# A decoder trunk: weight sums moved from VectorE to accumulating DMAs, and one set of transposes placed earlier

## The chip, the cores and the metric

The kernel runs on one NeuronCore of a Trainium2 chip. TensorE (PE) does matmuls and transposes, VectorE (DVE) and ScalarE (ACT) elementwise work, GpSimd (POOL) small scalar steps; SyncE (SP) issues DMAs and POOL issues others. Each engine takes its instructions in order from a queue of its own and waits on semaphores. The metric is the device time of one execution in microseconds. The time before is 2124.06 us, the median of three runs (2122.8 to 2125.29).

## The reference

Two layers, each of three residual steps with a layer norm behind them, on 512 positions of width 1024 in float32:

```python
for l in range(DEPTH):
    x = layer_norm(ALPHA * x + 0.5 * swiglu(x, ffn1_w13[l], ffn1_w2[l]), ln_g[l, 0], ln_b[l, 0])
    m = mixer(x, w_in[l], ...)
    x = layer_norm(ALPHA * x + m, ln_g[l, 1], ln_b[l, 1])
    x = layer_norm(ALPHA * x + 0.5 * swiglu(x, ffn2_w13[l], ffn2_w2[l]), ln_g[l, 2], ln_b[l, 2])

def swiglu(x, w13, w2):
    a, b = jnp.split(x @ w13, 2, axis=-1)
    return (jax.nn.silu(a) * b) @ w2          # inner width 2816
```

`mixer` projects x to eight parts, runs a gated linear recurrence on some and a gated spatial mixing on others, projects both branches, merges them by sigmoids and ends with one output projection.

## The kernel before

**Float32 products in three passes.** Every operand is split (`split`, L117) into a rounded high part, made by ScalarE (L118), and the rest, made by VectorE (L119). A product of two operands is then three matmuls: high by high, high by low, low by high. `weights` (L121) loads 128 x 1024 weights (512 KB) with SP into one of four `raw` buffers and splits them into two of ten `w` tiles.

**A SwiGLU stage** (`ffn`, L444) runs over 22 column blocks j of 128 inner columns. For each it loads two weight blocks, `a` and `b`, and computes `pa` and `pb` (`proj`, L143), 24 matmuls of 512 columns each; `glu` multiplies silu(`pa`) with `pb` and stores the result in quarters. Blocks j and j + 11 make one block k of the second product, and when the second of them is done, `activation_sums(k)` and `weight_sums(k)` follow. The order of k is 8, 9, 10, then 0 to 7.

**The second product** (class `Seven`) is a 2 x 2 block product with seven instead of eight block multiplications (Strassen's scheme in Winograd's form). It needs sums of the quarters of the second weights, `w2`: t1 = q0 + q1, t3 = q2 + q1, t2 = q0 + t3 and t4 = q3 + t2, where q0 to q3 are the four 128 x 512 quarters as they lie in DRAM. `weight_sums` (L278) loads them with SP into two tiles, `ra_w` and `rb_w`, forms the four sums on VectorE (L284, L289) and stores each with a DMA on POOL's queue (L285, L290) to the DRAM tiles `t1`, `t2` and `t34`. The tag of `ra_w` and `rb_w` has two buffers, so the next block's loads wait until this block's stores have landed. `run` (L331) later loads quarters and sums (`two`, L345) as `r_b`, `r_t`, `r_c` and `r_d`, splits and multiplies them.

**Between stages.** At the end of a stage four rows of 128 positions are finished one after the other. `norm` (L187) normalises a row (a square sum on ScalarE, two small steps on POOL, two on VectorE) and hands out `to_features` (L155), which transposes it on TensorE into `xh` and `xl`, the operands of the next stage. The next stage's first two pairs of blocks are computed in two halves of 256 columns: the first half needs rows 0 and 1, the second rows 2 and 3 (`need`, L209).

**What sets the order.** The class `Flow` keeps a clock in ns that advances by 216 per matmul of 512 columns as matmuls are written. Side work is a generator with a due time: `flow.add(gen, delay)` makes it due `delay` ns from now, each `tick` runs one due step, and `finish` runs what is left. Row transposes are due `LN_NS` = 11500 ns behind their `norm`. The program so written is then compiled, and the scheduler may set an instruction ahead of others on its engine where its operands allow it; semaphores keep the dependences.

Of the kernel before, what the change touches and what calls it, by code (L numbers as in the profile page):

```python
# [27 lines left out]
F32 = mybir.dt.float32  # L28
# [3 lines left out]
ALU = mybir.AluOpType  # L32
# [50 lines left out]
def trunk(ctx: ExitStack, tc, x_in, xt_in, w13, w2, w_in, w_br, w_out, ln_g, ln_b, lb_in, hgn, sgg, sgb, sgws,  # L83
# [37 lines left out]
    def weights(src, name, early=False):  # L121
# [8 lines left out]
        return hi, lo  # L130

    NW = 10
    NS, NRAW, NSA = 33, 4, 3
# [52 lines left out]

    def norm(t, xt, sums, g, b, last):  # L187

# [12 lines left out]
        if not last:  # L201
            x_at[t] = dram.tile([P, D], F32, name=f"xd{t}", tag=f"xd{t}", bufs=2)
            nc.gpsimd.dma_start(x_at[t], xt)
            ready[t] = flow.add(to_features(t, xt), LN_NS)

    LN_NS = 11500.0
    ready = [None] * NT
# [7 lines left out]
    def out_proj(nk, lhs, w_of, c, ln, tag):  # L215
# [23 lines left out]
        for t in range(NT):  # L239
            sums = small("sums", 2)  # L240
            for q in range(2):
                for k in range(nk - tail, nk):
                    unit(k, t, (q,))
                add_to(xs[t], q, c, ys[t][q], sums)
            norm(t, xs[t], sums, g, b, False)

# [12 lines left out]
    class Seven:  # L259
# [5 lines left out]
        def __init__(self, w_of):  # L265
            self.w_of = w_of
            self.r, self.t, self.last = {}, {}, None
            self.t1 = [dram.tile([P, 512], F32, name=f"t1{k}", tag=f"t1{k}", bufs=1) for k in range(NH2)]
            self.t2 = [dram.tile([P, 2, 512], F32, name=f"t2{k}", tag=f"t2{k}", bufs=1) for k in range(0, NH2, 2)]
            self.t34 = [dram.tile([P, 2, 512], F32, name=f"t34{k}", tag=f"t34{k}", bufs=1) for k in range(NH2)]  # L270

# [6 lines left out]
        def weight_sums(self, k):  # L278
# [5 lines left out]
            V.tensor_tensor(t1, a[:, 0], a[:, 1], op=ALU.add)  # L284
            nc.gpsimd.dma_start(self.t1[k], t1)  # L285
            for to, dst, u, v in ((self.t34[k][:, 0], a[:, 1], b[:, 0], a[:, 1]),
                                  (self.t2[k // 2][:, k % 2], a[:, 0], a[:, 0], a[:, 1]),
                                  (self.t34[k][:, 1], b[:, 1], b[:, 1], a[:, 0])):
                V.tensor_tensor(dst, u, v, op=ALU.add)  # L289
                nc.gpsimd.dma_start(to, dst)  # L290
# [40 lines left out]
        def run(self, c, ln, last):  # L331
# [45 lines left out]
            for k in ks:  # L377
                two(f"b{k}", [self.w_of(k)[:, 0], self.t1[k]], [("B11", k), ("t1", k)])
                if k % 2 == 0:
# [35 lines left out]
            for k in range(4):  # L415
                two(f"d{k}", [self.t34[k]], [("t3", k), ("t4", k)], True)
            if not last:
# [10 lines left out]
            for k in ks:  # L428
                if k >= 4:
                    two(f"d{k}", [self.t34[k]], [("t3", k), ("t4", k)])  # L430
                if k < NH2 - tail:
                    for ps, p in ((E, P7), (F, P4)):
                        for tt in range(2):
                            mm(ps, p, [k], tt, True, True)
# [8 lines left out]

    def ffn(l, i, last=False, first_of_all=False):  # L444
        made = list(range(Seven.KEPT, NH2)) + list(range(Seven.KEPT))
        seven = Seven(lambda k: w2[l, i, k])
        js = [j for k in made for j in (k, k + NH2)]
# [10 lines left out]
        def glu(j, args):  # L458
# [6 lines left out]
            if a:  # L465
                seven.activation_sums(k)
                seven.weight_sums(k)

# [9 lines left out]
        for z, j in enumerate(js[start:]):  # L478
# [9 lines left out]
            pair_of(j, args, 0, T)  # L488
            glu(j, args)
        seven.run(0.5 / ALPHA, (l, 2 * i), last)  # L490

# [375 lines left out]
    for l in range(DEPTH):  # L867
        ffn(l, 0, first_of_all=(l == 0))
        if l == 0:
            flow.finish(prep)  # L870
        mixer(l, lb, om)
        ffn(l, 1, last=(l == DEPTH - 1))

# [97 lines left out]
```

## Time and profile before

| what | us |
|---|---|
| median of three runs | 2124.06 |
| the profiled execution, its own time | 2122.98 |
| its span, first to last instruction | 2120.1 |
| TensorE busy in the span | 2097.9 |
| TensorE waiting for `xh` (3 times) | 11.0 |

The span has this course: in the first layer the first SwiGLU's blocks until about 262 us, its second product to about 357, the mixer to about 707, the second SwiGLU's blocks to about 950 and its second product to 1060; then the second layer in the same way. In a row of a timeline stand the start in us, the duration, engine, line, operation, output and inputs, shape and count, and in brackets how long the engine idled before and what ended it. SPq rows are DMA issues on SP; a DMA issue on POOL is an instruction of about 0.54 us. In a row of DMA issues the last two figures are the size and the median time from issue to landing. In a row of windows stand the busy time of each engine with its count, the granted clock, the DMA engines' busy share and GB/s.

### The profile page before, as it was taken

The page shows a single profiled execution, that of the slowest core. Times are in us where ns is not written, and L with a number is a line of the kernel's source. Part 1 is how long each engine was busy: PE and PEld are TensorE (multiplying, and loading weights), DVE is VectorE, ACT ScalarE, POOL GpSimd, SP SyncE. Part 2 cuts the span into 40 slices and gives each one's busy share as a digit, 9 for nine tenths or more (in the row PEclk, how much of TensorE's full clock was granted, in tenths as well). Part 3 has the DMA queues.
Part 4 walks back from the last instruction along what each step waited for, and adds up shares of the span by engine and source line. Part 5 has one row for each costly group of instructions (what it writes and reads, how often), then busy time and mean ns, then how long its engine had stood idle before and what let it go on. Part 6 is the DMA issues. An engine that isn't in the chain of part 4 may idle for free.

```text
span 2120.1 us, 26533 instructions
## 1 busy us (share of the span) xinstructions
PE 2097.9 (99%) x10024; PEld 1761.5 (83%) x10024; DVE 1226.6 (58%) x2019; ACT 772.2 (36%) x1090; POOL 214.6 (10%) x360
## 2 busy tenths in 40 slices
PE   8999999999999999999999999999999999999998
PEld 6888888888888888888898888888888888888886
DVE  5545578843535644548754456779344456454586
ACT  4222455224322422226522234552333324222363
POOL 0101002001000110101111010020010001110101
PEclk9999999999999999999999999999999999999999
DMA  7665777122242465557757557761222426655674
GB/s 268 215 209 179 251 254 263 42 80 80 82 157 90 162 235 185 192 207 275 249 186 235 179 203 237 273 227 42 89 89 89 141 90 202 211 192 201 224 262 143
DMA packets 113905, 381.01 MB, mean 180 GB/s; under 512 B 14321, under 2 KB 14577, under 8 KB 113777
## 3 DMA queue, kind: packets, MB, share of 16 engines
q1 hardware_dynamic: 88848, 291.68, 42.0%
q0 software_dynamic: 24928, 87.64, 10.9%
q8 instruction: 78, 1.28, 0.2%
q14 instruction: 51, 0.41, 0.1%
HBM read 311.11 MB, written 68.16 MB: 179 GB/s over the span
## 4 chain that ended last, share of the span: by engine, by line
PE 80%; DVE 2%; ACT 1%; DMA 1%; POOL 0%; issue 0%; POOLq 0%; DVEq 0%; ACTq 0%
PE pa L143 17%; PE pb L143 16%; PE z L143 8%; PE pA L341 4%; PE pC L341 4%; PE y L143 4%; PE y L226 3%; PE pF L341 2%; PE q L143 2%; PE pE L341 2%; PE f L143 2%; PE pB L341 2%; PE i L551 2%; PE g L143 2%; PE v L551 2%; PE u L143 2%
## 5 line engine op out<-in xcount | busy, mean ns | idle before, releaser
L143 PE MATMUL pa<-xh,h_a 128*128 128x512 f32 (+1 forms) x752 | 285.0, 379 | 11.2 <-ACT xh L118 11.0
L143 PE MATMUL pa<-xl,h_a 128*128 128x512 f32 (+1 forms) x752 | 284.6, 378 | 0.1
L143 PE MATMUL pa<-xh,l_a 128*128 128x512 f32 (+1 forms) x752 | 283.7, 377 | 0.0
L143 PE MATMUL pb<-xh,h_b 128*128 128x512 f32 (+1 forms) x752 | 283.1, 377 | 0.0
L143 PE MATMUL pb<-xh,l_b 128*128 128x512 f32 (+1 forms) x752 | 282.4, 376 | 0.3 <-DVE l_b L119 0.3
L143 PE MATMUL pb<-xl,h_b 128*128 128x512 f32 (+1 forms) x752 | 282.4, 375 | 0.0
L119 DVE TENSOR_TENSOR l_b<-r_b,h_b 128x1024 fp32r<-128x1024 f32 x132 | 161.5, 1224 | 166.4 <-ACT h_b L118 165.8
L118 ACT ACTIVATE h_b<-r_b 128x1024 fp32r<-128x1024 f32 x132 | 139.9, 1060 | 303.6 <-PE pa L143 245.4
L463 DVE TENSOR_TENSOR r<-sa,pb 128x512 f32<-128x512 f32 x88 | 60.5, 688 | 303.3 <-PE pb L143 303.3
L118 ACT ACTIVATE h_a<-r_a 128x1024 fp32r<-128x1024 f32 (+1 forms) x89 | 93.5, 1051 | 278.9 <-PE pb L143 264.2
L143 PEld LDWEIGHTS pa<-xh,h_a 128*128 128x128 f32 x752 | 142.9, 190 | 38.4 <-ACT xh L118 12.6
L143 PEld LDWEIGHTS pa<-xl,h_a 128*128 128x128 f32 x752 | 142.2, 189 | 28.0 <-DVE xl L119 2.3
L143 PEld LDWEIGHTS pa<-xh,l_a 128*128 128x128 f32 x752 | 142.4, 189 | 25.6
L143 PEld LDWEIGHTS pb<-xl,h_b 128*128 128x128 f32 x752 | 141.7, 188 | 25.8
L143 PEld LDWEIGHTS pb<-xh,l_b 128*128 128x128 f32 x752 | 141.6, 188 | 26.1 <-DVE l_b L119 0.8
L143 PEld LDWEIGHTS pb<-xh,h_b 128*128 128x128 f32 x752 | 141.7, 188 | 25.5
L119 DVE TENSOR_TENSOR l_a<-r_a,h_a 128x1024 fp32r<-128x1024 f32 (+1 forms) x89 | 107.7, 1210 | 16.2 <-ACT h_a L118 12.3
L143 PE MATMUL z<-xh,h_z 128*128 128x512 f32 x256 | 102.6, 401 | 0.0
L285 POOL DMA_DIRECT2D t<-t x44 | 23.9, 543 | 763.8 <-DVE t L284 697.5
L143 PE MATMUL z<-xh,l_z 128*128 128x512 f32 x256 | 99.8, 390 | 0.0
L143 PE MATMUL z<-xl,h_z 128*128 128x512 f32 x256 | 99.8, 390 | 0.0
L119 DVE TENSOR_TENSOR l_z<-r_z,h_z 128x1024 fp32r<-128x1024 f32 x32 | 39.2, 1225 | 72.5 <-ACT h_z L118 72.4
(270 smaller groups left out, 4246.5 us busy)
## 6 DMA issues: line engine op xcount, KB each, us to landing
r_b<-in_w_dram SPq DMA_DIRECT2D x88, 512.0 KB, 4.7
r_a<-in_w_dram SPq DMA_DIRECT2D x87, 512.0 KB, 4.7
ra_w<-in_w_dram SPq DMA_DIRECT2D x44, 512.0 KB, 5.5
rb_w<-in_w_dram SPq DMA_DIRECT2D x44, 512.0 KB, 5.2
t<-ra_w POOLq DMA_DIRECT2D x88, 256.0 KB, 2.6
r_c<-in_w_dram SPq DMA_DIRECT2D x44, 512.0 KB, 6.3
r_d<-t SPq DMA_DIRECT2D x44, 512.0 KB, 4.6
r_z<-in_w_in_dram SPq DMA_DIRECT2D x32, 512.0 KB, 3.5
```

What stands on the lines that cost most here:

```text
L118: S.activation(hi, src, AF.Copy)
L119: V.tensor_tensor(lo, src, hi.bitcast(F32), op=ALU.subtract)
L143: PE.matmul(ps[:, n0:n0 + n], a[:, cs], m[:, n0:n0 + n], start=(i == 0), stop=(i == 3 * nk - 1))
L226: PE.matmul(ys[t][q], a[:, ts], m[:, q * 512:(q + 1) * 512], start=(k == 0 and i == 0), stop=(k == nk - 1 and i == 2))
L285: nc.gpsimd.dma_start(self.t1[k], t1)
L341: PE.matmul(ps[tt], a[:, ts], m, start=(start and k == 0 and z == 0), stop=(stop and k == NH2 - 1 and z == 2), skip_group_check=not start)
L463: V.tensor_tensor(seven.part(k, a), sa.rearrange("p (h t) -> p h t", h=2), pb.rearrange("p (h t) -> p h t", h=2), op=ALU.mult)
L551: PE.matmul(pss[t], a[k // 2][:, k % 2, ts], m[:, cs], start=(k == 0 and i == 0), stop=(k == KT - 1 and i == 2))
```

## The change

Two things. First, for the second SwiGLU of each layer `weight_sums` is left out. A new generator, `sums_in_dram`, forms the same sums by DMAs on POOL's queue that read and write DRAM alone: a copy puts a first operand into the DRAM tile, and a second DMA with `accum_op` adds the other operand to it. Per block k these are six DMAs, each of which needs the one before: a copy of q0 and q2 into `t13` (512 KB), the addition of q1 to both, a copy of t3 into `t2` (256 KB), the addition of q0, a copy of t2 into `t4`, the addition of q3. The generator is handed to the `Flow` ahead of the mixer, due 4000 ns later, and takes four blocks at a time with 9000 ns between its steps. The DRAM tiles are arranged anew (`t13` for t1 and t3, `t4` alone), each with two buffers; `run` therefore loads t3 and t4 with two DMAs of 256 KB instead of one of 512 KB. Second, the delay of the row transposes behind the mixer's output projection is 9500 ns instead of 11500; elsewhere it stays.

```diff
@@ -129,6 +129,7 @@
         split(hi, lo, raw)
         return hi, lo
 
+    SUM_GAP = 9000.0
     NW = 10
     NS, NRAW, NSA = 33, 4, 3
 
@@ -184,7 +185,7 @@
         kw = {} if accum is None else {"accum_out": accum[:, q:q + 1]}
         V.scalar_tensor_tensor(xt[:, H[q]], v, c, xt[:, H[q]], op0=ALU.mult, op1=ALU.add, **kw)
 
-    def norm(t, xt, sums, g, b, last):
+    def norm(t, xt, sums, g, b, last, wait=11500.0):
 
 
         nm = small("nm")
@@ -201,9 +202,8 @@
         if not last:
             x_at[t] = dram.tile([P, D], F32, name=f"xd{t}", tag=f"xd{t}", bufs=2)
             nc.gpsimd.dma_start(x_at[t], xt)
-            ready[t] = flow.add(to_features(t, xt), LN_NS)
-
-    LN_NS = 11500.0
+            ready[t] = flow.add(to_features(t, xt), wait)
+
     ready = [None] * NT
 
     def need(*ts):
@@ -242,7 +242,7 @@
                 for k in range(nk - tail, nk):
                     unit(k, t, (q,))
                 add_to(xs[t], q, c, ys[t][q], sums)
-            norm(t, xs[t], sums, g, b, False)
+            norm(t, xs[t], sums, g, b, False, 9500.0)
 
     def load_rows():
         xs = []
@@ -265,9 +265,27 @@
         def __init__(self, w_of):
             self.w_of = w_of
             self.r, self.t, self.last = {}, {}, None
-            self.t1 = [dram.tile([P, 512], F32, name=f"t1{k}", tag=f"t1{k}", bufs=1) for k in range(NH2)]
-            self.t2 = [dram.tile([P, 2, 512], F32, name=f"t2{k}", tag=f"t2{k}", bufs=1) for k in range(0, NH2, 2)]
-            self.t34 = [dram.tile([P, 2, 512], F32, name=f"t34{k}", tag=f"t34{k}", bufs=1) for k in range(NH2)]
+            self.t13 = [dram.tile([P, 2, 512], F32, name=f"t13{k}", tag=f"t13{k}", bufs=2) for k in range(NH2)]
+            self.t2 = [dram.tile([P, 2, 512], F32, name=f"t2{k}", tag=f"t2{k}", bufs=2) for k in range(0, NH2, 2)]
+            self.t4 = [dram.tile([P, 512], F32, name=f"t4{k}", tag=f"t4{k}", bufs=2) for k in range(NH2)]
+
+        def sums_in_dram(self, group=4):
+
+            for k0 in range(0, NH2, group):
+                ks = range(k0, min(k0 + group, NH2))
+                w = {k: self.w_of(k) for k in ks}
+                t2 = {k: self.t2[k // 2][:, k % 2] for k in ks}
+                copies = (lambda k: (self.t13[k], w[k][:, 0:3:2]), lambda k: (t2[k], self.t13[k][:, 1]),
+                          lambda k: (self.t4[k], t2[k]))
+                adds = (lambda k: (self.t13[k], w[k][:, 1:2].broadcast_to([P, 2, 512])), lambda k: (t2[k], w[k][:, 0]),
+                        lambda k: (self.t4[k], w[k][:, 3]))
+                for copy, add in zip(copies, adds):
+                    for k in ks:
+                        nc.gpsimd.dma_start(*copy(k))
+                    yield 0.0, SUM_GAP
+                    for k in ks:
+                        nc.gpsimd.dma_start(*add(k), accum_op=ALU.add)
+                    yield 0.0, SUM_GAP
 
         def part(self, k, a):
 
@@ -282,10 +300,10 @@
             nc.sync.dma_start(a, w[:, 0:2])
             nc.sync.dma_start(b, w[:, 2:4])
             V.tensor_tensor(t1, a[:, 0], a[:, 1], op=ALU.add)
-            nc.gpsimd.dma_start(self.t1[k], t1)
-            for to, dst, u, v in ((self.t34[k][:, 0], a[:, 1], b[:, 0], a[:, 1]),
+            nc.gpsimd.dma_start(self.t13[k][:, 0], t1)
+            for to, dst, u, v in ((self.t13[k][:, 1], a[:, 1], b[:, 0], a[:, 1]),
                                   (self.t2[k // 2][:, k % 2], a[:, 0], a[:, 0], a[:, 1]),
-                                  (self.t34[k][:, 1], b[:, 1], b[:, 1], a[:, 0])):
+                                  (self.t4[k], b[:, 1], b[:, 1], a[:, 0])):
                 V.tensor_tensor(dst, u, v, op=ALU.add)
                 nc.gpsimd.dma_start(to, dst)
 
@@ -375,7 +393,7 @@
             tail = 2
             fetched = {k: self.fetched(k) for k in ks}
             for k in ks:
-                two(f"b{k}", [self.w_of(k)[:, 0], self.t1[k]], [("B11", k), ("t1", k)])
+                two(f"b{k}", [self.w_of(k)[:, 0], self.t13[k][:, 0]], [("B11", k), ("t1", k)])
                 if k % 2 == 0:
                     m = min(2, NH2 - k)
                     two(f"t2{k}", [self.t2[k // 2][:, 0:m]], [("t2", k + z) for z in range(m)])
@@ -413,7 +431,7 @@
                             mm(ps, p, ks[0:2] if k == 1 else [k], tt, False, True)
             g, b = ln_params(*ln)
             for k in range(4):
-                two(f"d{k}", [self.t34[k]], [("t3", k), ("t4", k)], True)
+                two(f"d{k}", [self.t13[k][:, 1], self.t4[k]], [("t3", k), ("t4", k)], True)
             if not last:
                 begin_features()
             sums = [small("sums", 2) for _ in range(NT)]
@@ -427,7 +445,7 @@
             tail = NW // 2
             for k in ks:
                 if k >= 4:
-                    two(f"d{k}", [self.t34[k]], [("t3", k), ("t4", k)])
+                    two(f"d{k}", [self.t13[k][:, 1], self.t4[k]], [("t3", k), ("t4", k)])
                 if k < NH2 - tail:
                     for ps, p in ((E, P7), (F, P4)):
                         for tt in range(2):
@@ -441,9 +459,8 @@
                 add_to(xs[t], 0, c, F[tt], sums[t])
                 norm(t, xs[t], sums[t], g, b, last)
 
-    def ffn(l, i, last=False, first_of_all=False):
+    def ffn(l, i, seven, last=False, first_of_all=False, sums=None):
         made = list(range(Seven.KEPT, NH2)) + list(range(Seven.KEPT))
-        seven = Seven(lambda k: w2[l, i, k])
         js = [j for k in made for j in (k, k + NH2)]
 
         def blocks(j, early=False):
@@ -464,7 +481,8 @@
                             pb.rearrange("p (h t) -> p h t", h=2), op=ALU.mult)
             if a:
                 seven.activation_sums(k)
-                seven.weight_sums(k)
+                if sums is None:
+                    seven.weight_sums(k)
 
         start = 0 if first_of_all else 2
         first = [blocks(j, True) for j in js[:start]]
@@ -487,6 +505,8 @@
                 args = blocks(j)
             pair_of(j, args, 0, T)
             glu(j, args)
+        if sums is not None:
+            flow.finish(sums)
         seven.run(0.5 / ALPHA, (l, 2 * i), last)
 
     def gates():
@@ -865,11 +885,13 @@
 
     prep = flow.add(prepare(), 30000.0)
     for l in range(DEPTH):
-        ffn(l, 0, first_of_all=(l == 0))
+        ffn(l, 0, Seven(lambda k: w2[l, 0, k]), first_of_all=(l == 0))
         if l == 0:
             flow.finish(prep)
+        seven = Seven(lambda k: w2[l, 1, k])
+        sums = flow.add(seven.sums_in_dram(), 4000.0)
         mixer(l, lb, om)
-        ffn(l, 1, last=(l == DEPTH - 1))
+        ffn(l, 1, seven, last=(l == DEPTH - 1), sums=sums)
 
 
 def _masks():
```

How the compiled program moves, at the places that matter. The first is POOL's queue in the first SwiGLU of the first layer, one block (k = 1): `t_76` is that block's DRAM tile of the first SwiGLU, `ra_w_929` and `rb_w_930` its loaded quarters. Before:

```order
L285 DMA t_76<-t_931 128x512
L290 DMA t_93<-ra_w_929 128x512
L290 DMA t_86<-ra_w_929 128x512
L290 DMA t_93<-rb_w_930 128x512
L285 DMA t_77<-t_1086 128x512
```

And now, where `t_2815`, `t_2825` and `t_2832` are the tiles `t13`, `t2` and `t4` of the second SwiGLU:

```order
L303 DMA t_76<-t_931 128x512
L284 DMA t_2815<-in_w_dram 256x512
L308 DMA t_76<-ra_w_929 128x512
L308 DMA t_86<-ra_w_929 128x512
L287 DMA t_2815<-in_w_dram 256x1x512
L308 DMA t_93<-rb_w_930 128x512
L284 DMA t_2825<-t_2815 128x512
L287 DMA t_2825<-in_w_dram 128x512
L284 DMA t_2832<-t_2825 128x512
L287 DMA t_2832<-in_w_dram 128x512
L303 DMA t_77<-t_1086 128x512
```

All 66 DMAs of a layer's sums stand in this way in the first SwiGLU of the same layer, one block's six in each of its eleven rounds; none stands in the mixer.

The second place is VectorE where the mixer ends and the second SwiGLU begins, first layer. Row 3 is `x_5324`, its normalising steps are L197 and L198; `l_a` and `l_b` are low parts of the next weight blocks, `xl` those of transposed rows. Before:

```order
L191 TENSOR_SCALAR nm<-sums 128x1
L119 TENSOR_TENSOR l_a_5603<-r_a_5600,h_a_5602 128x1024
L119 TENSOR_TENSOR l_b_5609<-r_b_5606,h_b_5608 128x1024
L197 SCALAR_TENSOR_TENSOR x_5324<-x_5324,nm,lng 128x512 x2
L198 SCALAR_TENSOR_TENSOR x_5324<-x_5324,rstd,lnb 128x512 x2
L119 TENSOR_TENSOR xl_5327<-tr_5653,xh_5326 128x2x128
L119 TENSOR_TENSOR xl_5331<-tr_5665,xh_5330 128x2x128
L119 TENSOR_TENSOR l_a_5880<-r_a_5877,h_a_5879 128x1024
```

Now, with row 3 as `x_5429` and the third pair's first block, `l_a_5880` above, as `l_a_5944`:

```order
L119 TENSOR_TENSOR l_b_5686<-r_b_5683,h_b_5685 128x1024
L192 TENSOR_SCALAR nm<-sums 128x1
L119 TENSOR_TENSOR l_a_5944<-r_a_5941,h_a_5943 128x1024
L119 TENSOR_TENSOR xl_5432<-tr_5712,xh_5431 128x2x128
L119 TENSOR_TENSOR l_b_5950<-r_b_5947,h_b_5949 128x1024
L198 SCALAR_TENSOR_TENSOR x_5429<-x_5429,nm,lng 128x512 x2
L199 SCALAR_TENSOR_TENSOR x_5429<-x_5429,rstd,lnb 128x512 x2
```

The third pair's first split now stands ahead of row 3's normalisation; it frees the `raw` buffer for the fifth `r_a` load.

The third is TensorE a little later, where row 3's transposes stand among the half-width matmuls. Before, they stood behind all of the first half:

```order
L143 MATMUL pb_5613<-xh_5332,h_b_5608 128x256
L143 MATMUL pb_5613<-xl_5333,h_b_5608 128x256
L143 MATMUL pb_5613<-xh_5332,l_b_5609 128x256
L161 MATMUL tr_5728<-ident,x_5324 128x128 x4
L161 MATMUL tr_5737<-ident,x_5324 128x128 x4
```

Now fifteen and twelve matmuls of that half follow them:

```order
L144 MATMUL pb_5690<-xl_5434,h_b_5685 128x256
L144 MATMUL pb_5690<-xh_5433,l_b_5686 128x256
L162 MATMUL tr_5802<-ident,x_5429 128x128 x4
L144 MATMUL pb_5690<-xh_5435,h_b_5685 128x256
L144 MATMUL pb_5690<-xl_5436,h_b_5685 128x256
```

On ScalarE the order just there is as it was: the `h_a` of the fifth pair's load stands directly ahead of the four evictions `xh` of row 3.

## The prediction

> **What bounds the kernel now.** I read the page's first part, then the list of waits of TensorE, then the windows by stage.
>
> ```profile
> PE 2097.9 (99%) x10024; PEld 1761.5 (83%) x10024; DVE 1226.6 (58%) x2019; ACT 772.2 (36%) x1090; POOL 214.6 (10%) x360
> PE pa L143 <- ACT xh L118: 11.0, 3, 5.6
> PE pE L341 <- DVE l_d L119: 0.7, 1, 0.7
> core 0: us, PE busy (x) PEld busy (x) DVE busy (x) ACT busy (x) POOL busy (x), PEclk, DMA share, GB/s
> 130.00:152.00 22.00, 22.00 (x99) 18.22 (x98) 10.90 (x16) 6.32 (x9) 2.17 (x4) 1.00 0.57 190
> 357.00:500.00 143.00, 142.96 (x801) 124.55 (x800) 90.58 (x240) 45.25 (x72) 5.70 (x9) 1.00 0.26 85
> ```
>
> TensorE is busy in 99% of the span and waits 12 us in all, 5.6 of them for the first load. In the steady stages it is full at clock 1.00. VectorE and the DMA queues, from which the change takes work, bound nothing: whatever leaves them is worth nothing unless it ends a wait of TensorE. Two of the three waits for `xh` lie where the mixer ends and the second SwiGLU begins, one per layer. The timeline of TensorE there, and the chain's first full-width block behind it (first layer, second layer, and for comparison the end of the first layer, where the same 192 half-width matmuls and 16 transposes stand):
>
> ```profile
> 706.77 0.28 PE L143 MATMUL pa<-xh,h_a 128*128 128x256 f32 x1
> 719.36 1.04 PE L161 MATMUL tr<-ident,x 128*128 128x128 f32 x8
> 723.25 0.58 PE L143 MATMUL pa<-xh,h_a 128*128 128x256 f32 x1 [2.86 <-ACT xh L118]
> 736.90 5.24 PE pa L143 x23
> ...
> 1759.46 0.28 PE L143 MATMUL pa<-xh,h_a 128*128 128x256 f32 x1
> 1775.66 0.39 PE L143 MATMUL pa<-xh,h_a 128*128 128x256 f32 x1 [2.58 <-ACT xh L118]
> 1788.28 5.24 PE pa L143 x23
> ...
> 1060.72 0.28 PE L143 MATMUL pa<-xh,h_a 128*128 128x256 f32 x1
> 1086.18 5.24 PE pa L143 x23
> ```
>
> From the first half-width matmul to the first full block the stretch takes 30.13, 28.82 and 25.46 us. The two mixer ends thus lose 4.67 + 3.36 = 8.0 us against the third: the waits, and matmuls that run slower just behind them. That is all that the change can win. What made the wait, on SP, VectorE and ScalarE:
>
> ```profile
> 703.88 1.41 DVE L198 SCALAR_TENSOR_TENSOR x<-x,rstd,lnb 128x512 f32<-128x512 f32 x2 [0.46 <-POOL rstd L170]
> 712.60 1.41 DVE L198 SCALAR_TENSOR_TENSOR x<-x,rstd,lnb 128x512 f32<-128x512 f32 x2
> 714.59 1.22 DVE L119 TENSOR_TENSOR l_a<-r_a,h_a 128x1024 fp32r<-128x1024 f32 x1
> 715.84 0.33 SPq L124 DMA_DIRECT2D r_a<-in_w_dram  x1
> 721.87 1.06 ACT L118 ACTIVATE h_a<-r_a 128x1024 fp32r<-128x1024 f32 x1 [3.16 <-DMA r_a<-in_w_dram]
> 722.83 0.64 ACT L118 ACTIVATE xh<-tr 128x256 fp32r<-128x256 f32 x2
> ```
>
> Row 3 was normalised by 714.01, but its eight transposes stand behind all the half-width matmuls (719.36), and their evictions `xh` stand on ScalarE behind an `h_a` that waits for its load. That load went out at 715.84, when VectorE's `l_a` freed a buffer; this `l_a` stood behind row 3's normalisation.
>
> **The transposes (9500 in place of 11500).** No instruction is added. Row 3's transposes move from behind 96 half-width matmuls to behind 81 and 84, some 1.4 to 1.8 us (12 to 15 times 0.12) earlier. The new order on VectorE also puts the `l_a` that frees the buffer ahead of row 3's two normalising steps, so the load leaves about 3 to 4 us earlier; by the same 6.03 us from issue (715.84) to `h_a` (721.87) it lands near 718, about when the transposes are done. The second half of the matmuls should then find its `xh` in time. I do not take the full 8.0: `h_a` still stands just before the four `xh` on ScalarE, and its `l_a` (1.22 us) stands between the four `xl` on VectorE. I leave 0.75 us a layer, so **6.5 us won**. Bounds: 8.0 at best. At worst nothing, or a loss: row 2's transposes now stand 7 half-width matmuls behind 706.77, at 707.6; its last step ended at 705.29, and two splits of 1.2 us are new in front of it, so 707.7; another us of lateness costs 2 x 1.1 = 2.2.
>
> **Where the sums go.** By the diff they are handed out during the mixer. The compiled order says otherwise: POOL's queue has all six DMAs of a block in the *first* SwiGLU of the same layer, between that stage's own stores, since nothing that they need is made later. The trace shows the same for another DMA that the program writes in the mixer:
>
> ```profile
> L529 POOL DMA_DIRECT2D hg<-in_hgn_dram x2: 547/639/731, 1.2 to 475.1; - x2
> ```
>
> It went out at 1.2 us, some 350 us ahead of the mixer, which begins near 357. So I cost the sums in the first SwiGLU. In the second one they remove 44 loads on SP, 88 stores on POOL and 88 additions on VectorE, all of them behind a full TensorE, worth nothing. The `d` loads become two of 256 KB (44 loads more on SP, 0.33 us each); TensorE waited for a `d` tile once, 0.7 us, and I add nothing.
>
> In the first SwiGLU one block k takes four projections, and this is its round on POOL, SP, VectorE and ScalarE:
>
> ```profile
> 121.61 0.54 POOL L285 DMA_DIRECT2D t<-t  x1 [16.67 <-DVE t L284]
> 126.16 0.54 POOL L290 DMA_DIRECT2D t<-rb_w  x1 [1.20 <-DVE rb_w L289]
> 143.37 0.54 POOL L285 DMA_DIRECT2D t<-t  x1 [16.66 <-DVE t L284]
> 130.28 0.33 SPq L283 DMA_DIRECT2D rb_w<-in_w_dram  x1
> 143.66 0.68 DVE L289 TENSOR_TENSOR ra_w<-rb_w,ra_w 128x512 f32<-128x512 f32 x1
> 141.02 1.06 ACT L118 ACTIVATE h_a<-r_a 128x1024 fp32r<-128x1024 f32 x1 [3.90 <-PE pb L143]
> 145.80 1.22 DVE L119 TENSOR_TENSOR l_a<-r_a,h_a 128x1024 fp32r<-128x1024 f32 x1
> ```
>
> A round is 143.37 - 121.61 = 21.76 us, and POOL idles 16.7 of it. The new chain in it is serial, each DMA on POOL's queue waiting for the one before to land: copy of 512 KB, add of 512, copy of 256, add of 256, copy of 256, add of 256 (its landing is awaited by nobody there). Nothing in the trace copies DRAM to DRAM or adds in a DMA. The nearest rows are the same stage's (100 to 240 us), and one store of 512 KB from the whole run:
>
> ```profile
> r_a<-in_w_dram SPq DMA_DIRECT2D x10, 512.0 KB, 4.2
> t<-ra_w POOLq DMA_DIRECT2D x14, 256.0 KB, 2.5
> ra_w<-in_w_dram SPq DMA_DIRECT2D x7, 512.0 KB, 5.7
> rb_w<-in_w_dram SPq DMA_DIRECT2D x7, 512.0 KB, 5.1
> t<-t POOLq DMA_DIRECT2D x7, 256.0 KB, 2.3
> t<-rb_w POOLq DMA_DIRECT2D x7, 256.0 KB, 4.1
> ...
> xd<-x POOLq DMA_DIRECT2D x20, 512.0 KB, 3.1
> ```
>
> Low: 0.54 (first store's issue) + 4.2 + 4.2 + 3 x 2.3 + 0.54 = 16.4 us. High, with an add at twice a copy: 0.54 + 5.7 + 11.4 + 4.1 + 8.2 + 4.1 + 0.54 = 34.6. I take copies in the middle (4.9 and 3.3) and adds a quarter dearer (6.1 and 4.1), because from 256 to 512 KB a store grew only from 2.5 to 3.1: 0.54 + 4.9 + 6.1 + 3.3 + 4.1 + 3.3 + 0.54 = **22.8 us**. That is 1.0 more than the round, so POOL falls back 1.0 us a round, over ten gaps of eleven rounds 10 us.
>
> What covers it: the store of `rb_w` stands behind the first add, so it goes at 121.61 + 0.54 + 4.9 + 0.54 = 127.6 instead of 126.16; SP's load of the next `rb_w` left at 130.28, took 5.1, and is used at 143.66, which leaves 8.3 - 1.4 = 6.9 us. After that VectorE waits in its queue, and with it the splits behind it. But ScalarE waits for TensorE to free weight tiles (3.90 above): ten tiles are five blocks, so a split that ended at 147.02 for a place freed at 141.0 has 4 x 5.44 - 6.0 = 15.7 us before TensorE wants it (5.44 = a quarter round). Together 22.6 us: TensorE stands still only if the chain exceeds 21.76 + 22.6 / 10 = **24.0 us**. At 22.8 it is hidden. The DMA share, 0.57 at 190 GB/s, rises by some 2 MB on 4.2 MB (adds reading one more): 0.57 x (1 + 0.5 to 0.75) = 0.86 to 1.0. That is the reason why the cover is thin.
>
> **Sum.** Against the profiled execution: 2122.98 - 6.5 = 2116.5 (span 2120.1 to 2113.6). The median shown is 1.1 above that execution: **2117.5 us**.
>
> **Rivals.** *First, the chain is longer than 24.0 us* and POOL becomes the bound of the first SwiGLU: each us beyond costs ten a layer. At 27: 10 x 5.24 - 22.6 = 29.8 a layer, 60 - 6.5, so 2177; at the high bound 34.6, 10 x 12.84 - 22.6 = 105.8 a layer, near 2329. For it: a store that meets loads takes 4.1 instead of 2.5 us, the share above, and five landings in series. Against: POOL's 16.7 us idle and the cover. An add that takes twice its copy, since it reads two rows for each that it writes, is the case in it with a price of its own: 0.54 + 4.9 + 9.8 + 3.3 + 6.6 + 3.3 + 0.54 = 29.0, 49.8 a layer, 2217. Chance of the rival 0.30, of which the doubled add 0.10.
> The Trainium skill ("Collectives: The Full Stack", The bandwidth ceiling) has that rule: the arithmetic costs no cycles, but the add "needs **two source reads**", and this halved the rate of a ring's reducing half. No run here shows it yet; stores of 256 and 512 KB say that much of a short DMA's time is no transfer.
> *Second, the stall stays*: `h_a`, or VectorE's splits, hold the four `xh` as before, and the time is 2122 to 2125. For it: the order on ScalarE before the last four `xh` is unchanged. Against: the load that it waits for leaves earlier. Chance 0.14.
> *Third, the sums do run in the mixer*, as the words say; there the DMA share is 0.26 and the copies are free, so again 2117.5. Against it the order; chance 0.03.
>
> **Chances and range.** The forecast has 0.53. Of this kernel about 0.2% (4.2 us) can be told from no change. Faster: forecast and third rival, 0.56; same: 0.14; slower: 0.30. The forecast's own range is 2115 to 2121. The range for 8 in 10 begins at 2113.5 (the whole 8.0 won and two more) and takes in the first rival up to a chain of 26.4 us: 2 x (46.4 - 22.6) = 47.5 above the forecast, 2165.
>
> **What would show it.** The transposes: no wait of `pa` for `xh` near 720 and 1772, and 25.5 to 26.5 us from the first half-width matmul to the first full block. The chain: POOL's `t` stores in the first SwiGLU still 21.76 apart, the waits of `t` for VectorE shrunk from 16.7 to near nothing. Copies and adds: landings of about 4.9, 6.1, 3.3 and 4.1. The forecast is wrong if `pa` or `pb` waits for `l_a`, `l_b` or their loads between 40 and 260 or 1090 and 1310; if rounds grow longer than 21.76, their excess gives the chain's length.

## The result: 232 us slower

The changed kernel takes 2357.01 us (median of four runs, 2354.37 to 2361.87) against 2124.68 us for the kernel before on the same chip: a ratio of 1.1101, with an interval of 1.1084 to 1.1117. The forecast was 2117.5 us, with a range up to 2165. It was wrong in sign and size, and the first rival's mechanism is what happened: the sums' chain on POOL's queue became the bound of the first SwiGLU.

Where the time went is read from TensorE's timeline, by the first matmul of each stage (the last one to the end of the span). The execution profiled after the change is the one of 2361.87 us, with a span of 2360.1 us against 2120.1 before. Lengths in us:

| stage | before, layer 1 | after | before, layer 2 | after |
|---|---|---|---|---|
| first SwiGLU, blocks | 244.24 | 316.36 | 242.70 | 308.23 |
| first SwiGLU, second product | 107.69 | 163.06 | 106.80 | 161.07 |
| mixer | 349.23 | 349.19 | 349.24 | 349.20 |
| second SwiGLU, blocks | 247.14 | 242.65 | 245.83 | 242.65 |
| second SwiGLU, second product | 106.81 | 107.78 | 114.82 | 114.22 |

The first SwiGLU, from which the change removes nothing, is 127.5 and 119.8 us longer. The second one's blocks are 7.7 us shorter in sum.

### The profile page after: what moved, and what is told of

Its sections match the earlier page's. It is cut to its first block, busy times and chain, and to the rows that moved or that the text cites. A ratio compares the mean times of both kernels' runs of the same rounds, so it can differ in the third digit from the quotient of the medians.

```text
span 2360.1 us, 26341 instructions
## 1 busy us (share of the span) xinstructions
PE 2143.4 (91%) x10024; PEld 1788.0 (76%) x10024; DVE 1175.0 (50%) x1931; ACT 767.6 (33%) x1090; POOL 262.3 (11%) x404
## 4 chain that ended last, share of the span: by engine, by line
PE 33%; issue 9%; DMA 5%; POOL 2%; DVE 1%; ACT 0%; POOLq 0%; DVEq 0%; ACTq 0%
PE pa L144 6%; PE pb L144 6%; DMA t<-in_w_dram 4%; PE z L144 4%; PE pC L359 2%; PE pA L359 2%; PE y L226 2%; PE y L144 2%; PE pF L359 1%; PE pE L359 1%; PE f L144 1%; PE q L144 1%; PE i L571 1%; PE g L144 1%; PE v L571 1%
## 5 line engine op out<-in xcount | busy, mean ns | idle before, releaser
L144 PE MATMUL pa<-xh,l_a 128*128 128x512 f32 (+1 forms) x752 | 295.0, 392 | 110.4 <-DVE l_a L119 110.4
L144 PE MATMUL pa<-xh,h_a 128*128 128x512 f32 (+1 forms) x752 | 293.1, 390 | 6.1 <-ACT xh L118 6.1
L144 PE MATMUL pa<-xl,h_a 128*128 128x512 f32 (+1 forms) x752 | 292.4, 389 | 0.2 <-DVE xl L119 0.2
L144 PEld LDWEIGHTS pa<-xh,l_a 128*128 128x128 f32 x752 | 148.2, 197 | 142.8 <-DVE l_a L119 115.5
L144 PEld LDWEIGHTS pa<-xh,h_a 128*128 128x128 f32 x752 | 148.0, 197 | 34.4 <-ACT xh L118 7.3
L144 PEld LDWEIGHTS pa<-xl,h_a 128*128 128x128 f32 x752 | 147.4, 196 | 30.3 <-DVE xl L119 2.3
L144 PEld LDWEIGHTS pb<-xh,h_b 128*128 128x128 f32 x752 | 141.4, 188 | 25.5
L302 DVE TENSOR_TENSOR t<-ra_w 128x512 f32<-128x512 f32 x22 | 15.2, 691 | 181.3 <-DMA ra_w<-in_w_dram 181.3
L287 POOL DMA_DIRECT2D t<-in_w_dram x66 | 61.2, 928 | 313.5 <-DMA t<-t 199.2
```

The source lines that it names most:

```text
L144: PE.matmul(ps[:, n0:n0 + n], a[:, cs], m[:, n0:n0 + n], start=(i == 0), stop=(i == 3 * nk - 1))
L287: nc.gpsimd.dma_start(*add(k), accum_op=ALU.add)
```

## The profile after

The first line of the page's first part:

```profile
PE 2143.4 (91%) x10024; PEld 1788.0 (76%) x10024; DVE 1175.0 (50%) x1931; ACT 767.6 (33%) x1090; POOL 262.3 (11%) x404
```

The list of waits of TensorE (us in total, times, longest us):

```profile
PE pa L144 <- DVE l_a L119: 110.4, 12, 12.5
PE pB L359 <- DVE l_t L119: 42.4, 4, 21.2
PE pA L359 <- DVE l_b L119: 20.6, 2, 11.0
PE pB L359 <- ACT h_t L118: 15.0, 2, 7.7
PE pC L359 <- DVE x L186: 11.3, 2, 6.2
PE pa L144 <- ACT xh L118: 6.1, 2, 5.7
```

TensorE fell from 99% to 91% busy. The two new large groups are `pa` waiting for a split `l_a` of the blocks, and the second product (`pA`, `pB`) waiting for splits of fetched sums. VectorE, the engine named, has less to do than before (1175.0 us against 1226.6); what it waits for in turn are the loads of a block's quarters (L300, L301), which SP cannot issue before the stores of the block ahead have landed; and those stand on POOL's queue. From VectorE's own list of waits, and from SP's:

```profile
DVE t L302 <- DMA ra_w<-in_w_dram: 181.3, 18, 14.1
SPq L300 <- DMA t<-ra_w: 283.4, 25, 20.6
```

Before, the longest wait of this load (L282 there) for such a store was 6.9 us, and all of them came to 69.0 us over twice as many blocks. The waits of TensorE above come to 206 us, against 12 before; the rest of the 240 us of the longer span is slower matmuls (2143.4 - 2097.9 = 45.5 us more busy time for the same 10024). POOL's timeline over one round of the first SwiGLU (start, duration, engine, line, operation, tiles; in brackets the idle time before it and what ended it; L303 and L308 are the stage's own stores, L284 the copies and L287 the additions of the sums):

```profile
136.37 0.86 POOL L303 DMA_DIRECT2D t<-t  x1
136.94 0.86 POOL L284 DMA_DIRECT2D t<-in_w_dram  x1
137.62 1.24 POOL L308 DMA_DIRECT2D t<-ra_w  x2
144.40 1.10 POOL L287 DMA_DIRECT2D t<-in_w_dram  x1 [5.53 <-DMA t<-in_w_dram]
144.99 1.08 POOL L308 DMA_DIRECT2D t<-rb_w  x1
153.00 0.54 POOL L284 DMA_DIRECT2D t<-t  x1 [6.93 <-DMA t<-in_w_dram]
158.93 0.86 POOL L287 DMA_DIRECT2D t<-in_w_dram  x1 [5.38 <-DMA t<-t]
164.48 0.54 POOL L284 DMA_DIRECT2D t<-t  x1 [4.69 <-DMA t<-in_w_dram]
169.87 0.81 POOL L287 DMA_DIRECT2D t<-in_w_dram  x1 [4.85 <-DMA t<-t]
170.42 0.84 POOL L303 DMA_DIRECT2D t<-t  x1
```

From one L303 store to the next a round takes 170.42 - 136.37 = 34.05 us; it took 21.76 before. POOL does little in it, but the chain leaves no gap: five landings in series, 7.5, 8.6, 5.9, 5.6 and 5.4 us. Each of these, from the issue of one DMA of the chain to the issue of the next, is called a link below. The L303 stores no longer wait for VectorE; VectorE waits for them. The DMA issues of the same stage, 40 to 360 us (size, median us from issue to landing):

```profile
t<-in_w_dram POOLq DMA_DIRECT2D x19, 512.0 KB, 7.6
ra_w<-in_w_dram SPq DMA_DIRECT2D x10, 512.0 KB, 6.9
t<-in_w_dram POOLq DMA_DIRECT2D x19, 256.0 KB, 5.3
t<-ra_w POOLq DMA_DIRECT2D x18, 256.0 KB, 7.2
t<-rb_w POOLq DMA_DIRECT2D x9, 256.0 KB, 8.1
```

The stage's own stores and loads grew as well: `t<-ra_w` and `t<-rb_w` from 2.5 and 4.1 to 7.2 and 8.1 us, `ra_w` from 5.7 to 6.9.

Call lag how much later a round's L303 store goes out than the same store before. When it reaches TensorE, the windows show (busy us of each engine with its count, granted clock, DMA engines' busy share, GB/s):

```profile
60.00:110.00 50.00, 50.00 (x222) 41.40 (x222) 16.65 (x24) 10.41 (x14) 13.32 (x22) 1.00 0.70 208
110.00:160.00 50.00, 34.25 (x138) 27.43 (x136) 12.69 (x20) 7.97 (x11) 8.59 (x13) 0.86 0.71 195
```

TensorE is full until 110 us and then stands still for about a third of the time. The third and fourth of these stores before, then POOL's first, third and last L303 of the layer after, and TensorE's first wait in the steady blocks:

```profile
78.09 0.54 POOL L285 DMA_DIRECT2D t<-t  x1 [16.67 <-DVE t L284]
99.85 0.54 POOL L285 DMA_DIRECT2D t<-t  x1 [16.67 <-DVE t L284]
...
33.99 0.56 POOL L303 DMA_DIRECT2D t<-t  x1 [32.01 <-DVE t L302]
101.91 0.85 POOL L303 DMA_DIRECT2D t<-t  x1
375.33 0.84 POOL L303 DMA_DIRECT2D t<-t  x1
```

```profile
126.65 0.79 PE L144 MATMUL pa<-xh,l_a 128*128 128x512 f32 x1 [7.28 <-DVE l_a L119]
```

The third store is now 23.8 us late and the fourth (136.37) 36.5, and between the two TensorE stops (126.65 - 7.28 = 119.4). The last store goes out at 375.33, and ten rounds of 34.13 us are 123.7 us more than ten of 21.76: nearly the 127.5 by which the stage grew.

The transposes did what they should. The first half-width matmul and the first full block's first matmul, both layers:

```profile
834.29 0.28 PE L144 MATMUL pa<-xh,h_a 128*128 128x256 f32 x1
859.31 0.40 PE L144 MATMUL pa<-xh,h_a 128*128 128x512 f32 x1
...
2003.22 0.28 PE L144 MATMUL pa<-xh,h_a 128*128 128x256 f32 x1
2028.25 0.40 PE L144 MATMUL pa<-xh,h_a 128*128 128x512 f32 x1
```

25.0 us each, a little less than the 25.5 to 26.5 expected, with no wait of `pa` for `xh` there.

## Experiments

The theory formed from the two traces: the sums' chain on POOL's queue, in the first SwiGLU, is longer than that stage's round, and everything behind it in the queue falls back. Rivals for the cause: the bytes that these DMAs add, the additions by themselves, and the stage's own load on the DMA engines.

**The transposes alone.** The kernel before with nothing but the shorter delay:

```diff
-    def norm(t, xt, sums, g, b, last):
+    def norm(t, xt, sums, g, b, last, wait=11500.0):
-            ready[t] = flow.add(to_features(t, xt), LN_NS)
+            ready[t] = flow.add(to_features(t, xt), wait)
-            norm(t, xs[t], sums, g, b, False)
+            norm(t, xs[t], sums, g, b, False, 9500.0)
```

> The kernel before with the 9500 ns alone, no sums by DMA. In the changed kernel the second SwiGLU's blocks took 242.65 us in both layers against 247.14 and 245.83 before, 7.7 us together. If the earlier transposes made this, the two stages are 242.5 to 243.5 again and the time is 2116 to 2118. If it came from the loads and additions that left that stage, they stay at 245 or more and the time is 2121 to 2125.

Measured: 2115.95 us against 2122.97 before, a ratio of 0.9968 (0.9955 to 0.998). The second SwiGLU's blocks take 242.84 us in both layers. Its list of waits has one wait of `pa` for `xh` left, that of the first load:

```profile
PE pa L143 <- ACT xh L118: 5.8, 1, 5.8
```

So this edit is worth 7 us by itself (the interval leaves no change out), and needs no load or addition to be gone.

**The sums alone.** The changed kernel with 11500 everywhere:

```diff
-            norm(t, xs[t], sums, g, b, False, 9500.0)
+            norm(t, xs[t], sums, g, b, False)
```

> The sums by DMA alone, transposes at 11500 everywhere. If the two edits are independent: 2357.0 + 7.0 = 2364, second SwiGLU's blocks at 245.8 to 247.2 instead of 242.65. If the DMAs alone also removed the stall (fewer loads and additions there): about 2357.

Measured in a single run: 2346.93 us, neither number. The second SwiGLU's blocks are at 244.67 and 244.56: the sums alone had already taken 2.5 and 1.3 us of the wait away, so the edits overlap and the transposes add about 2 us a layer on top. By that this kernel should be 4 us slower than the changed one; it was 7 us faster than the fastest run of that kernel and 15 faster than its profiled one. The difference to the profiled one lies in the first SwiGLU, 19 us shorter over both layers (its blocks 305.92 instead of 316.36 in the first), where both kernels have the same instructions in the same order on every engine: the same chain took 32.7 us a round here and 34.1 there. What differs was not found out; the changed kernel's own four runs lie within 7.5 us of each other.

**The sums where the diff puts them.** The scheduler is told to keep the sums' DMAs in the order of the program:

```diff
-                        nc.gpsimd.dma_start(*copy(k))
+                        tc.keep_in_program_order(nc.gpsimd.dma_start(*copy(k)))
...
-                        nc.gpsimd.dma_start(*add(k), accum_op=ALU.add)
+                        tc.keep_in_program_order(nc.gpsimd.dma_start(*add(k), accum_op=ALU.add))
```

Of a layer's 66, 58 now stand in the mixer; the first eight, the copies and first additions of four blocks, still stand in the first SwiGLU.

> The changed kernel with the sums' DMAs kept in the order in which the program writes them: most stand in the mixer on POOL's queue, one block group's copies and first adds late in the first SwiGLU. If the place is the cause (rounds of the first SwiGLU that POOL cannot keep), the first SwiGLU's blocks are 244 and 243 us and its second product 107 again, the mixer's 349 us stay, and the time is 2115 to 2122. If the chain costs wherever it stands, because POOL's small steps of the mixer wait behind it, the mixer is 10 us or more longer in each layer and the time is above 2140.

Measured: 2115.56 us, a ratio of 0.9966 (0.9952 to 0.9979). The first SwiGLU is back at 244.15 and 107.66 us, the mixer stays at 349.20, and TensorE's waits are two rows:

```profile
PE pa L144 <- ACT xh L118: 6.1, 2, 5.6
PE pE L359 <- DVE l_d L119: 0.8, 2, 0.6
```

The same DMAs cost some 240 us in one place and nothing in the other. In the mixer they also gain nothing: the interval is that of the transposes alone.

**No additions.** Each accumulating DMA is replaced by a plain copy of the same size, so the second SwiGLU's sums are not formed:

```diff
-                        nc.gpsimd.dma_start(*add(k), accum_op=ALU.add)
+                        nc.gpsimd.dma_start(*add(k))
```

> The changed kernel with each adding DMA a plain copy of the same operand and size, so the second SwiGLU's sums are wrong; same number of DMAs, same waits. If reading and writing back in the adds is the price, the round on POOL falls from 34.1 us to 24 or less and the time to 2125 or less. If the copies from DRAM to DRAM land as late as the adds (in the changed kernel a round has 7.4, 8.6, 5.9, 5.6 and 5.4 us from link to link, copies first, third and fifth), the round stays above 31 us and the time above 2300.

Measured in a single run: 2272.65 us, between what the two theories expected. POOL's L303 stores, the first and the tenth:

```profile
34.38 0.56 POOL L303 DMA_DIRECT2D t<-t  x1 [32.41 <-DVE t L302]
297.25 0.57 POOL L303 DMA_DIRECT2D t<-t  x1 [2.18 <-DVE r L480]
```

Nine rounds of 29.2 us: the additions are 5 of the 12.4 us by which a round is too long, and copies alone are too long as well.

**The stage's own stores past the chain.** The first SwiGLU's sum stores are issued by SP instead of POOL:

```diff
-            nc.gpsimd.dma_start(self.t13[k][:, 0], t1)
+            nc.sync.dma_start(self.t13[k][:, 0], t1)
-                nc.gpsimd.dma_start(to, dst)
+                nc.sync.dma_start(to, dst)
```

> The changed kernel with the first SwiGLU's own sums stored from SP's queue instead of POOL's; the sums' chain keeps POOL's queue. If sharing the in-order queue is the cause, the first SwiGLU's blocks fall from 316 and 308 us to 242 to 255, though the chain's rounds stay near or above 28 us; what POOL has to do behind the chain (row loads, the norm's steps) comes late instead, so that stage's second product is still up to 60 us longer and the time is 2120 to 2260. If the DMA engines' load is the cause, the blocks stay at 300 or more and the time above 2300.

Measured in a single run: 2333.63 us. The blocks are back at 246.95 and 242.68 us, with TensorE at full clock though the DMA share is higher, but the second product takes 216.29 and 214.78. The window of 40 to 260 us:

```profile
40.00:260.00 220.00, 220.00 (x973) 182.21 (x972) 111.50 (x163) 64.02 (x82) 29.58 (x41) 1.00 0.88 262
```

The first row of TensorE's waits:

```profile
PE pC L359 <- DVE x L186: 202.2, 2, 101.8
```

`pC` waits for a row `x` that POOL loads (L251) at the stage's end, now behind the rest of the chain. The first such load before, and in this run:

```profile
275.06 0.54 POOL L251 DMA_DIRECT2D x<-in_x_dram  x1 [17.80 <-ACT s L118]
...
394.79 2.43 POOL L251 DMA_DIRECT2D x<-in_x_dram  x4
```

So the stall of the blocks comes from POOL's queue and not from the load on the DMA engines; a queue that is 120 us late stops whatever is next in it. The second product was expected to lose 60 us at most and lost 108, so the time also missed its range.

**The same six DMAs, not in series.** The copies into `t2` and `t4` read the weights instead of the sums just made. The bytes stay; the sums of the second SwiGLU are not the scheme's:

```diff
-                copies = (lambda k: (self.t13[k], w[k][:, 0:3:2]), lambda k: (t2[k], self.t13[k][:, 1]),
-                          lambda k: (self.t4[k], t2[k]))
+                copies = (lambda k: (self.t13[k], w[k][:, 0:3:2]), lambda k: (t2[k], w[k][:, 2]),
+                          lambda k: (self.t4[k], w[k][:, 0]))
```

> The same six DMAs per block of the same sizes, in the same place (POOL's queue in the first SwiGLU), but the copies into t2 and t4 read the weights instead of the sums just made, so that no copy waits for an addition. The sums of the second SwiGLU are no longer the scheme's; the bytes moved are the same. Theory S (the series of landings is what fills POOL's round): per block only two landings stand in series, about 7.4 for the copy of 512 KB and about 6 for the copies of 256 KB, with issues some 17 us, below the round of 21.76; blocks and second product return to 244 and 107 us and the time to 2115 to 2125. Theory B (the bytes that DMAs from DRAM to DRAM add are the bound): the bytes are the same, so the round stays at 28 us or more, and the time above 2250.

Measured in a single run: 2144.39 us, 213 of the 232 us gone, yet 19 above theory S's range. Blocks 245.37 and 242.70, second product 126.06 and 118.26. The window of 40 to 260 us:

```profile
40.00:260.00 220.00, 220.00 (x972) 182.24 (x971) 103.38 (x151) 59.82 (x78) 64.70 (x99) 1.00 0.94 279
```

POOL's first and eleventh L303:

```profile
35.47 0.56 POOL L303 DMA_DIRECT2D t<-t  x1 [33.49 <-DVE t L302]
270.69 0.87 POOL L303 DMA_DIRECT2D t<-t  x1
```

Ten rounds of 23.5 us, still 1.8 too long. The long ones are those in which the compiled order puts eight of the sums' DMAs (from the fourth round on 25.2 to 28.3 us, against 20.3 to 21.9 for those with four). That `t2` is one tile for two blocks may be why they are bunched so and still wait for one another; no run shows it. In the end the queue is 18 us late, and the second product of that layer is 18.4 us longer.

**Both.** Is what is left POOL's time per round (theory C) or the load of 0.94 (theory R)? The copies that do not read sums and the copies in place of additions together (e5_apart and e4_noadd in the expectation), so that the sums are not formed:

> e4_noadd and e5_apart together: the copies into t2 and t4 read the weights, and the additions are plain copies of the same size (the sums of the second SwiGLU are not formed). Theory C (POOL's time per round, whatever makes it up, is the bound, and lag beyond 21.76 us is paid in full): e5_apart's rounds were 24.3 us on the mean, additions cost 6 us of a round in e4_noadd; so rounds fall below 21.76, first SwiGLU's blocks and second product return to 244 and 107, time 2115 to 2119. Theory R (what is left in e5_apart, 20 and 13 us in the two second products, comes from the DMA engines' load of 0.94, with bytes that hardly change here): second product still 118 or more, time 2135 or more.

Measured in a single run: 2117.58 us; blocks 244.98 and 242.70, second product 109.95 and 107.43. The window of 40 to 260 us:

```profile
40.00:260.00 220.00, 220.00 (x973) 182.21 (x972) 111.17 (x163) 64.24 (x82) 58.21 (x106) 1.00 0.89 303
```

POOL's first and eleventh L303:

```profile
35.10 0.56 POOL L303 DMA_DIRECT2D t<-t  x1 [33.13 <-DVE t L302]
254.63 0.56 POOL L303 DMA_DIRECT2D t<-t  x1
```

Rounds of 21.95 us, with the DMA engines at 0.89 and 303 GB/s, more than in any other kernel here, and TensorE full. Theory C's numbers came out, and theory R's did not. The share fell a little too, from 0.94 to 0.89, though the rate rose from 279 to 303 GB/s, so it is not excluded that a share of 0.94 lengthened some landings of the run before. (By the rows above, the rounds not in series were 23.5 us and the additions 5 us of a round, not 24.3 and 6 as the expectation has them.) Over four kernels, the changed one and those without additions, not in series, and both, the first layer grew by 127.5, 79.3, 19.5 and 3.0 us, where the rounds give 10 x (34.13, 29.2, 23.5, 21.95 less 21.76) = 123.7, 74, 17 and 1.9.

**A link in the mixer.** To price the chain where less else runs (a DMA share of 0.26 in the mixer before, against 0.57 in the first SwiGLU, by the prediction's rows), the sums are kept in the mixer and made one block at a time:

```diff
-    SUM_GAP = 9000.0
+    SUM_GAP = 4500.0
-        def sums_in_dram(self, group=4):
+        def sums_in_dram(self, group=1):
```

(on top of the edit that keeps them in the program's order, e3_written in the expectation)

> The sums are kept in the mixer as in e3_written, but one block at a time with 4.5 us between steps, so that most links of the chain run alone beside the mixer's thinner loads. Time 2114 to 2118 under every theory. Read from it: the length of a link when it runs alone. Theory L (the landings in the first SwiGLU were long because of that stage's own loads and stores): copy of 512 KB below 5.5 us, copy of 256 KB below 4, additions about a quarter above. Theory D (a DMA from DRAM to DRAM takes that long by itself): copy of 512 KB 6.5 to 7.5, its addition 8 to 9, copies and additions of 256 KB 5 to 6.

Measured in a single run: 2115.63 us. One block's chain on POOL:

```profile
620.01 0.85 POOL L284 DMA_DIRECT2D t<-in_w_dram  x1
627.24 1.05 POOL L287 DMA_DIRECT2D t<-in_w_dram  x1 [6.38 <-DMA t<-in_w_dram]
635.11 0.55 POOL L284 DMA_DIRECT2D t<-t  x1 [6.81 <-DMA t<-in_w_dram]
638.69 0.82 POOL L287 DMA_DIRECT2D t<-in_w_dram  x1 [3.04 <-DMA t<-t]
644.16 0.54 POOL L284 DMA_DIRECT2D t<-t  x1 [4.65 <-DMA t<-in_w_dram]
647.29 0.82 POOL L287 DMA_DIRECT2D t<-in_w_dram  x1 [2.58 <-DMA t<-t]
```

Links of 7.2, 7.9, 3.6, 5.5 and 3.1 us: 27.3, and 27.8 to the next block. The medians over the 22 blocks of both layers, of which 20 are made wholly in the mixer, are close to these: 7.2, 7.4, 3.4, 6.1 and 3.8. The DMAs of 512 KB are nearly as long as in the first SwiGLU (7.5 and 8.6 there), near what theory D expected; the copies of 256 KB are shorter (3.6 and 3.1 against 5.9 and 5.4), as theory L did. So of the 34.05 us about 28 are what the chain takes in the mixer, and 6 come on top in the first SwiGLU. The mixer has loads of its own, so the 28 are not shown to be the chain's alone.

## Why the prediction was wrong, and where it was right

**What bounds the kernel, and the ceiling.** Right: TensorE alone, and 8.0 us at the end of the mixer. 7.7 us were won there, 7.0 in the run of that edit alone; the forecast was 6.5. Of the 0.75 us a layer held back for `h_a` and the splits hardly any was lost.

**Where the sums go.** Right, and it decides the result: all 66 DMAs of a layer ran in the first SwiGLU, as the compiled order said. The run that keeps them in the mixer shows that the place is the cause, and that the third rival's 2117.5 us is near what the program as written gives (2115.56).

**The chain's length: the step that failed.** Taken 22.8 us, measured 34.05. The terms, as the prediction put them, with the two measurements:

| link | taken | in the mixer | in the first SwiGLU |
|---|---|---|---|
| copy, 512 KB | 4.9 | 7.2 | 7.5 |
| addition, 512 KB | 6.1 | 7.9 | 8.6 |
| copy, 256 KB | 3.3 | 3.6 | 5.9 |
| addition, 256 KB | 4.1 | 5.5 | 5.6 |
| copy, 256 KB | 3.3 | 3.1 | 5.4 |

Two errors add up. The large DMAs were priced by loads and stores between DRAM and the core's own memory (4.2 to 5.7 us for 512 KB); from DRAM to DRAM a link took 7.2 in the mixer too. The sentence that little is paid for size (2.5 against 3.1 us for stores) does not carry over: a copy of twice the size took twice as long (7.2 against 3.1 and 3.6). And the rows that served as prices were medians of the stage *before* the change; with the chain in it the stage's own stores went from 2.5 to 7.2 us, and the chain's copies of 256 KB took 5.9 and 5.4. With 34.05 in its place the prediction's own sum gives 10 x 12.29 - 22.6 = 100.3 us a layer instead of nothing; the second error of the sum, the 22.6, is taken up below. That the upper bound of 34.6 us came so near is luck: it has doubled additions, which did not occur.

**The doubled addition.** It did not show as priced. In the first SwiGLU an addition took 1.15 times the copy for 512 KB and about the same for 256 KB. In the mixer it was 1.1 times for 512 KB, but 1.5 to 1.8 times for 256 KB; there the two read different sources (the copies a sum, the additions the weights). The run without additions has plain copies of the same operands in the same places: they landed in 6.0 us (512 KB) and in 5.4 and 4.0 us (256 KB, the second and the last), medians over both layers, where the additions took 8.2, 5.6 and 5.3. That is 1.0 to 1.4 times, and a round without additions was still 29.2 us. The Trainium skill ("Collectives: The Full Stack", The bandwidth ceiling) puts the halved rate of a ring's reducing half down to an add's two source reads; these single DMAs do not show a halved rate.

**The cover of 22.6 us.** Half right, and the second step that failed. TensorE first stopped when the lag lay between 23.8 and 36.5 us, which a cover of 22.6 allows. But the cover only delays: the second product needs the sums, so the whole lag was paid, part in the blocks and part there. Where the six DMAs were not in series, a lag of 18.5 us, inside the cover, left the blocks 1.1 us longer and the second product 18.4. In the four kernels compared above no cover is left over, and the threshold is the round itself, 21.76 us, not 24.0. The first rival's own sum, 10 x 12.84 - 22.6, came out at 105.8 a layer. With the measured round and no cover taken off, the sum is 123.7 for the first layer, and 127.5 was measured.

**The DMA share.** Foreseen at 0.86 to 1.0 and called the reason why the cover is thin. It was 0.70 in the stalled stage, since the chain stretched it, and 0.89 in the run without additions or series, where TensorE did not wait in the blocks. The share was not the limit of the changed kernel; the landings in series in one queue were.

**The chances.** The first rival had 0.30 and the forecast 0.53. With the bounds 16.4 and 34.6 on the chain and a round of 21.76, most of the interval lay above the round. The value taken, 22.8, lies below the middle of these bounds (25.5) and only 1.2 us below a threshold that rested on the cover. A value that close to its threshold, for an operation of which the trace had no row at all, gave no ground to call the other side less likely.

## What to carry to other kernels

Where a compiler orders the queues, read which stage a DMA is issued in before you price it: the same DMAs were free where 58 of a layer's 66 stood in the mixer, and cost 120 us a layer where all stood in the first SwiGLU. A chain of DMAs in which each waits for the last is priced by its landings in series against the round of the queue that it stands in, and all that is behind it in that queue is late with it; buffers ahead delay that price but do not lower it. An operation of which the trace has no row is given the range that its bounds allow, and if a threshold lies within them, its chances too.

## What the runs showed that was not expected

From DRAM to DRAM, 512 KB took 6.9 us from issue to landing (the median of copies and additions in the mixer of the run that makes one block at a time), where loads of that size beside them landed in 3.6 us (the median of `r_z`):

```profile
t<-in_w_dram POOLq DMA_DIRECT2D x18, 512.0 KB, 6.9
r_z<-in_w_in_dram SPq DMA_DIRECT2D x16, 512.0 KB, 3.6
```

The issue of an accumulating DMA on POOL takes 0.81 to 1.10 us instead of 0.54, and in the rounds quoted above a plain store issued just behind one shows 0.84 to 1.08 too. And TensorE, which stood still for a third of the window from 110 to 160 us, was granted a clock of 0.86 in it, against 1.00 where it is full. So its list of waits, 206 us, shows less than the stall's whole length: 45.5 us of it are matmuls that run slower. The prediction counted this at the mixer's ends (8.0 us for 5.4 us of waits there), and its first rival, priced by POOL's rounds, did not need it.
